# All 22 gate-and-up blocks by seven products, four first halves ahead

## The chip, the cores and the metric

The kernel runs on one core of a Trainium2 chip. The metric is the device time of one execution in microseconds (us). A profile of one execution gives each instruction's engine, start and duration. The engines are PE (TensorE, the matmuls), DVE (VectorE), ACT (ScalarE), POOL (GpSimd) and SP (SyncE, which issues all the DMAs of this kernel). Each engine works through its own instructions in a fixed order and waits for the others by semaphores.

## The reference

One encoder layer over 1024 positions of width 1024, in float32. A long first part (projections, a convolution mixer and a delta-rule mixer) ends in an output projection and a residual add. The change lies in the SwiGLU block that follows:

```python
y = jax.nn.sigmoid(gate_a) * y_conv + jax.nn.sigmoid(gate_b) * y_delta
x = x + y @ w_o[i]

h = rms_norm(x, g_ffn[i])
gt, up = split_cols(h @ w_gate_up[i], (D_FF, D_FF))
x = x + (jax.nn.silu(gt) * up) @ w_down[i]
...
return rms_norm(x, g_final)
```

`D_FF` is 2816, which is 22 blocks of 128 columns each for gate and for up.

## The kernel before

**Tiles.** Activations stand transposed, channels on partitions: `xT[b]` has the 128 channels of block b (8 of them) and 1024 positions, worked on in two halves h of 512. A matmul takes a 128x128 weight and a 128x512 activation. For float32 accuracy every operand is split into a rounded part (hi, a CAST on ACT, L712) and the rest (lo, a subtraction on DVE, L713), and `mm3` (L760) multiplies hi·hi, hi·lo and lo·hi: three matmuls for each 128-deep piece. The third is the one that takes the weight's lo; the second takes the activation's lo.

**Seven products.** A block of gate and up is a 2x2 problem: input channels 0-511 and 512-1023 (r), gate and up columns, times the two position halves. `gate_up` (L1736) does it in a Strassen form, with seven products of weights against the activation forms `B11`, `B21`, `B22`, `T1`, `T2`, `T3`, `T4`, each 4 pieces deep: 7 x 4 x 3 = 84 matmuls. The T forms are running differences of the four quarters of the normalised activation; `sums_of` (L1810) makes a form piece by piece, one DVE subtraction for the difference, then a CAST on ACT and a subtraction on DVE for the split. A plain block (`plain`, L1713) does the same with four products of 8 pieces over `B11`, `B21`, `B12`, `B22`: 96 matmuls, half of them for each position half.

**The beginning of this stage.** The output projection (`wo`, L1634 on) is finished for half 0 first. So `B11` and `B21` (half 0) are ready while `wo` still works on half 1; everything else needs half 1, which becomes available after the last residual add (`resid`, L1608), the norm (`Norm.finish`, L1489, called at L1652) and eight multiplications on DVE (L1656). To bridge this, the kernel before runs the work that needs half 0 alone: `plain(0, 0, ...)`, half of block 0 (48 matmuls), and `first_half` (L1726) of blocks 1 to 3, which are the two products `B11` and `B21` of each (24 matmuls per block). `GU_AHEAD` is the number of such blocks. Then come `plain(0, 1, ...)` with `B12` and `B22` (48 matmuls), the other five products of blocks 1 to 3, and 18 whole blocks. Forms are made on first use:

```python
while acts[0] is None:
    pn.sec = "gu.x"
    sums_of(*coming.pop(0))
    pn.sec = "gu"
```

with `coming` (L1816) in the order T1, T3, B22, T2, T4. In the early blocks the products are taken in that order too (L1741 to L1763).

**Weights.** `part_w` (L1694) loads a 512x128 piece of `w_gate_up` (256 KB) into one of four `raw` or four `rawb` (tile `mid`) buffers; DVE forms sums of the pieces (`s`, `a21`, `a12` in `gate_up`); `split_w` (L1500) splits the result into one of six `w` tiles. So each product has one CAST on ACT and one subtraction on DVE for its weight.

**Order.** `Plan.order` (L347) is a list scheduler with its own table of costs; it runs when the kernel is built, and its result is a fixed order per engine. Lower levels of a key go first, then earlier program order among what it expects to be ready. On the chip nothing is reordered: an instruction whose input is late holds up all that stand behind it on its engine.

Of the kernel before, what the change touches and what calls it, by code (L numbers as in the profile page):

```python
# [576 lines left out]
NS = sum(PAIRS)  # L577
HID_CAP, DF_CAP = 3, 24
GU_BANKS = 8
GU_AHEAD = 3  # L580
OT_AFTER = (4, 7, 10, 12)
WO_AFTER = 13
RE_CAP = 3
# [7 lines left out]
START = (("norm", 0), ("turn", 0, 0, 1), ("rows", 0), ("turn", 0, 1, 8), ("scale", 0, 0, 8),  # L591
         ("norm", 1), ("turn", 1, 0, 1), ("rows", 1), ("turn", 1, 1, 8), ("scale", 1, 0, 8))
PLE_BANKS = (2, 2)
GU_PLAIN = 1
X_AHEAD = 3
LN_KEPT = ()
ROWS_DMA = (0,)
# [27 lines left out]
def hybrid_block(tc, x, p, g_mix, w_in, conv_dw_w, conv_dw_b,  # L625
# [874 lines left out]
    def split_w(src):  # L1500
        t = wp.tile([P, 2, HK, P], F32R, tag="w", line="w", cap=N_W, stream="rest")
        split(t[:, 0], t[:, 1], src)
        return t
# [190 lines left out]
    def part_w(r, c, line):  # L1694

        t = mid.tile([P, HK, P], tag="raw", bufs=4, line=line, cap=4, stream="rest") if line == "raw" else \
            mid.tile([P, HK, P], tag="mid", line=line, cap=4)
        rows_ = w_gate_up[0][r * HK * P:(r + 1) * HK * P, c:c + P]
        pn.dma(t, rows_.rearrange("(k q) c -> q k c", q=P), also=[mark])
        return t  # L1700
# [12 lines left out]
    def plain(fb, h, w, acts):  # L1713

        ps = [gu_bank(), gu_bank()]
        for i in range(2):
            for k in range(KB):
                t = w[2 * i + k // HK]
                mm3(ps[i], t[:, 0, k % HK], t[:, 1, k % HK], *acts[k // HK][k % HK], k == 0, k == KB - 1)
        e = (hid_tile(fb) if h == 0 else hid[fb])[:, h]  # L1720
        pn.act(e, ps[0], AF.Silu)
        pn.tt(e, ps[1], e, ALU.mult)
        if h == 1:
            hidden(fb)

    def first_half(a11, a12):  # L1726

        p1 = mid.tile([P, HW], tag="m2", line="p1", bufs=4)
        pn.act(p1, product(a11, B11))
        yield  # L1730
        g0 = mid.tile([P, HW], tag="lnb", line="g0", bufs=3)
        pn.tt(g0, product(a12, B21), p1, ALU.add)
        pn.act(g0, g0, AF.Silu)
        yield p1, g0
# [64 lines left out]
    ws = []  # L1799
    for fb in range(GU_PLAIN):  # L1800
        ws.append([split_w(part_w(r, c + fb * P, "raw")) for c in (0, FF) for r in range(2)])
        plain(fb, 0, ws[fb], (B11, B21))
    ahead = {}
    for fb in range(GU_PLAIN, GU_PLAIN + GU_AHEAD):
        it = first_half(part_w(0, fb * P, "raw"), part_w(1, fb * P, "rawb"))
# [11 lines left out]

    if GU_PLAIN:
        for k in range(HK):
# [4 lines left out]
        pn.sec = "gu"  # L1824
        for fb in range(GU_PLAIN):
            plain(fb, 1, ws[fb], (B12, B22))
    for fb in range(GU_PLAIN, NF):
        gate_up(fb, ahead.get(fb))
# [231 lines left out]
```

## Time and profile before

| | us |
|---|---|
| median of 3 runs (2058.62 to 2061.99) | 2059.98 |
| the profiled execution | 2064.42 |
| its span, first to last instruction | 2062.7 |
| PE busy | 2032.3 |
| DVE busy | 1593.3 |
| ACT busy | 1115.1 |
| `w_gate_up` loads, first to last issue | 1292.5 to 1685.1 |

Times inside the execution count from the start of the span. A busy share is an average: whether an engine limits a stage is read from the stretch in which it works, and the change concerns a stretch of some 60 us from about 1300 us on. Matmuls overlap in the records: one of 128x512 is recorded with some 400 to 480 ns, and what counts is how often one starts.

### The profile page before, as it was taken

Reading aid. Unit: us, or ns where it says so; the run is one execution under the profiler, and the core shown is the slowest. Engines: PE = TensorE matmul, PEld = TensorE weight load, DVE = VectorE, ACT = ScalarE, POOL = GpSimd, SP = SyncE. Lnnn points to the kernel's source line nnn. Section 1 sums busy time; section 2 is a strip of 40 time slices with the busy share of each in tenths; the row PEclk is TensorE's granted clock in tenths of the full one; section 3 lists DMA queues with packets and bytes.
Section 4 is the critical chain, followed back from the end, with each engine's and each line's share of the span. In section 5 each row is a group of like instructions: output and inputs, shape, how many; then the busy total and the mean of one; then the engine's idle time right before and its main releaser. Section 6 shows DMA issues by size and latency. Waiting matters only on the chain.

```text
span 2062.7 us, 29058 instructions
## 1 busy us (share of the span) xinstructions
PE 2032.3 (99%) x9985; PEld 1670.3 (81%) x9985; DVE 1593.3 (77%) x2814; ACT 1115.1 (54%) x2629; POOL 129.8 (6%) x211
## 2 busy tenths in 40 slices
PE   9999999999999999999999999999999999999998
PEld 6887788888887888888888778888888888887887
DVE  6548999777968999998488876796656657989955
ACT  7635674566766675757875454433333335434462
POOL 1000111001100210012100000000000000000010
PEclk9999999999999999999999999999999999999999
DMA  6432432443333332544488676433323328534232
GB/s 209 153 101 93 133 108 92 147 139 108 118 117 114 111 94 98 189 128 133 159 277 268 206 248 194 143 113 117 98 87 120 100 86 290 165 109 135 85 108 102
DMA packets 278754, 288.61 MB, mean 140 GB/s; under 512 B 17767, under 2 KB 196128, under 8 KB 278606
## 3 DMA queue, kind: packets, MB, share of 16 engines
q1 hardware_dynamic: 278606, 286.76, 43.3%
q8 instruction: 78, 1.28, 0.3%
q14 instruction: 70, 0.57, 0.1%
HBM read 201.16 MB, written 85.53 MB: 139 GB/s over the span
## 4 chain that ended last, share of the span: by engine, by line
PE 51%; DVE 4%; ACT 1%; DMA 1%; issue 1%; SPq 0%; POOLq 0%; DVEq 0%; ACTq 0%
PE ps L244 50%; DVE big L292 2%; ACT big L269 1%; DVE mid L292 1%; DMA big<-d 1%; DMA mid<-d 1%; PE ps L249 0%; DVE w L292 0%; ACT w L269 0%; DVE m L292 0%; SPq L341 0%; DMA d<-mid 0%; ACT big L276 0%; ACT m L276 0%; ACT mid L276 0%
## 5 line engine op out<-in xcount | busy, mean ns | idle before, releaser
L244 PE MATMUL ps<-big,w 128*128 128x512 f32 x6972 | 1708.6, 398 | 4.5 <-ACT big L269 1.6
L244 PEld LDWEIGHTS ps<-big,w 128*128 128x128 f32 x6972 | 1285.4, 188 | 291.7 <-ACT mid L269 6.1
L269 ACT CAST w<-raw 128x512 fp32r<-128x512 f32 (+2 forms) x298 | 176.9, 597 | 258.3 <-PE ps L244 216.9
L292 DVE SCALAR_TENSOR_TENSOR big<-big,taps 128x512 f32<-128x512 f32 (+1 forms) x344 | 300.4, 907 | 12.3 <-ACT big L276 8.3
L292 DVE TENSOR_TENSOR w<-raw,w 128x512 fp32r<-128x512 f32 (+2 forms) x298 | 198.0, 667 | 83.1 <-ACT w L269 81.8
L269 ACT CAST w<-mid 128x512 fp32r<-128x512 f32 (+2 forms) x205 | 113.6, 559 | 145.3 <-PE ps L244 104.4
L292 DVE TENSOR_TENSOR big<-big 128x512 fp32r<-128x512 f32 (+4 forms) x259 | 177.1, 705 | 12.0 <-ACT big L269 5.1
L292 DVE TENSOR_TENSOR w<-mid,w 128x512 fp32r<-128x512 f32 (+2 forms) x205 | 123.9, 609 | 55.9 <-ACT w L269 55.1
L292 DVE TENSOR_TENSOR big<-ps,big 128x512 f32<-128x512 f32 (+1 forms) x172 | 117.4, 686 | 30.3 <-PE ps L244 21.3
L269 ACT CAST big<-big 128x512 fp32r<-128x512 f32 x162 | 95.8, 623 | 48.1 <-DVE big L292 31.1
L269 ACT COPY big<-big 32x128 f32<-32x128 f32 (+1 forms) x264 | 104.5, 443 | 22.7 <-DVE big L292 19.8
L269 ACT COPY big<-ps 128x512 f32<-128x512 f32 (+3 forms) x194 | 83.8, 445 | 54.5 <-PE ps L244 42.9
L244 PEld LDWEIGHTS ps<-big 128*128 128x128 f32 x706 | 99.5, 192 | 16.6 <-issue 5.7
L244 PE MATMUL ps<-big 128*128 128x128 f32 (+2 forms) x706 | 109.2, 299 | 3.1 <-ACT big L269 2.7
L292 DVE SCALAR_TENSOR_TENSOR big<-big,cw31s 128x512 f32<-128x512 f32 x120 | 93.3, 778 | 9.5 <-ACT big L276 7.5
L244 PE MATMUL ps<-w,big 128*128 128x512 f32 (+1 forms) x294 | 80.3, 403 | 0.0
L269 ACT COPY mid<-ps 128x512 f32<-128x512 f32 x72 | 42.0, 587 | 67.7 <-PE ps L244 58.2
L244 PEld LDWEIGHTS ps<-S,big 128*128 128x128 f32 x448 | 68.9, 190 | 10.8 <-DVE S L292 4.5
L244 PE MATMUL ps<-S,big 128*128 128x128 f32 x448 | 77.0, 277 | 0.0
L244 PEld LDWEIGHTS ps<-big,m 128*128 128x128 f32 x512 | 61.5, 191 | 10.2 <-ACT m L276 8.4
L244 PE MATMUL ps<-big,m 128*128 128x128 f32 x512 | 66.1, 279 | 1.0 <-ACT m L276 1.0
L276 ACT ACTIVATE big<-big 128x1024 f32<-128x1024 f32 (+2 forms) x80 | 56.7, 717 | 17.1 <-DVE big L292 13.4
(185 smaller groups left out, 1777.2 us busy)
## 6 DMA issues: line engine op xcount, KB each, us to landing
raw<-in_w_in_dram SPq DMA_DIRECT2D x128, 256.0 KB, 2.9
mid<-d SPq DMA_DIRECT2D x128, 256.0 KB, 3.7
d<-big SPq DMA_DIRECT2D x122, 256.0 KB, 3.2
big<-d SPq DMA_DIRECT2D x118, 256.0 KB, 5.3
d<-mid SPq DMA_DIRECT2D x99, 256.0 KB, 2.2
big<-dqkv SPq DMA_DIRECT2D x32, 512.0 KB, 5.2
raw<-in_w_gate_up_dram SPq DMA_DIRECT2D x49, 256.0 KB, 3.1
dqkv<-big SPq DMA_DIRECT2D x24, 512.0 KB, 2.6
```

The costliest lines, as they stand in the source:

```text
L244: o = self.add("pe", lambda: self.nc.tensor.matmul(out.ap(), lhsT.ap(), rhs.ap(), start=start, stop=stop, **kw), [out], [lhsT, rhs], cost)
L269: return self.nc.scalar.copy(out.ap(), in_.ap())
L276: return self.nc.scalar.activation(out.ap(), in_.ap(), func, **kw)
L292: return getattr(e, name)(**{k: v.ap() if isinstance(v, View) else v for k, v in kw.items()})
```

## The change

Two constants. Block 0 is no longer plain, and four blocks' `first_half` go ahead instead of three.

```diff
-GU_AHEAD = 3
+GU_AHEAD = 4
...
-GU_PLAIN = 1
+GU_PLAIN = 0
```

The loops over `range(GU_PLAIN)` (L1800, L1825) are then empty, `first_half` runs for blocks 0 to 3, `B12` is never made, and `B22` is made when its product in block 0 asks for it (L1823 no longer removes it from `coming`). Blocks 4 to 21 are whole blocks as before. On PE the plain block's 96 matmuls become 84.

What the constants move is told by the order of the built programs. The first place is DVE, about the last residual add (the `SCALAR_TENSOR_TENSOR big<-ps,mid`) and the norm behind it (`nrs`). Before:

```order
L292 SCALAR_TENSOR_TENSOR big<-ps,mid 128x512
L292 TENSOR_TENSOR w<-mid,w 128x512
L292 TENSOR_TENSOR lnb<-lnb,mid 128x512
L292 TENSOR_TENSOR mid<-raw,mid 128x512
L292 TENSOR_TENSOR raw<-raw 128x512
L292 TENSOR_SCALAR nrs<-ps 128x4
```

Now:

```order
L292 TENSOR_TENSOR mid<-raw,mid 128x512
L292 TENSOR_TENSOR raw<-raw 128x512
L292 SCALAR_TENSOR_TENSOR big<-ps,mid 128x512
L292 TENSOR_TENSOR w<-mid,w 128x512
L292 TENSOR_TENSOR lnb<-lnb,mid 128x512
L292 TENSOR_SCALAR nrs<-ps 128x4
L292 TENSOR_TENSOR w<-raw,w 128x512
```

The two weight sums of the first seven-product block (`mid<-raw,mid` is s = a21 + a22) have moved ahead of the residual add, and a weight split stands between `nrs` and the eight multiplications.

The second place is DVE again, from the making of the last pieces of T2 and T4 on (`big<-big`), with `w<-` the weight splits and `ps` results being combined. Before, where T4 is finished:

```order
L292 TENSOR_TENSOR w<-mid,w 128x512
L292 TENSOR_TENSOR big<-big 128x512 x3
L292 TENSOR_TENSOR big<-ps,big 128x512
L292 TENSOR_TENSOR big<-big 128x512 x7
L292 TENSOR_TENSOR mid<-raw,mid 128x512 x2
L292 TENSOR_TENSOR raw<-raw 128x512
L292 TENSOR_TENSOR w<-mid,w 128x512
```

Now (tile `m_13008` is p1 of block 0, into which its products are added):

```order
L292 TENSOR_TENSOR big<-big 128x512
L292 TENSOR_TENSOR big<-ps,big 128x512
L292 TENSOR_TENSOR m_13008<-ps,m_13008 128x512
L292 TENSOR_TENSOR big<-big 128x512
L292 TENSOR_TENSOR m_13008<-ps,m_13008 128x512
L292 TENSOR_TENSOR big<-big 128x512
L292 TENSOR_TENSOR w<-mid,w 128x512
L292 TENSOR_TENSOR big<-big,m_13008 128x512
L292 TENSOR_TENSOR big<-big 128x512
L292 TENSOR_TENSOR raw<-raw 128x512
L292 TENSOR_TENSOR mid<-mid,raw 128x512
L292 TENSOR_TENSOR big<-ps,big 128x512
```

Block 0's combinations now stand between the pieces of T4; before, T4 was made in one stretch and no seven-product block was being combined yet.

The third place is PE, at the end of T4 of the first seven-product block (`w_13225`, sums in `ps_13286`; buffer numbers kept, since the rows would read alike). Now:

```order
L244 MATMUL ps_13286<-big_13280,w_13225 128x512
L244 MATMUL ps_13290<-big_13100,w_13230 128x512 x2
L244 MATMUL ps_13286<-big_13280,w_13225 128x512 x2
L244 MATMUL ps_13286<-big_13288,w_13225 128x512 x3
L244 MATMUL ps_13286<-big_13304,w_13225 128x512 x3
L244 MATMUL ps_13290<-big_13100,w_13230 128x512
L244 MATMUL ps_13286<-big_13315,w_13225 128x512
L244 MATMUL ps_13290<-big_13111,w_13230 128x512 x3
L244 MATMUL ps_13290<-big_13116,w_13230 128x512
L244 MATMUL ps_13286<-big_13315,w_13225 128x512 x2
```

Before, the matmuls at this many places behind the norm belong to the second half of the plain block, in sequence:

```order
L244 MATMUL ps_13279<-big_13035,w_12915 128x512 x3
L244 MATMUL ps_13279<-big_13043,w_12915 128x512 x3
L244 MATMUL ps_13279<-big_13053,w_12915 128x512 x3
L244 MATMUL ps_13279<-big_13063,w_12915 128x512 x3
L244 MATMUL ps_13279<-big_13067,w_12934 128x512 x3
```

Block 1's first late product (T1, into `ps_13290`) is now interleaved with block 0's T4, matmul by matmul.

## The prediction

> **What bounds the kernel now.** First the page's busy shares and its chain that ended last, then that chain about the stage that changes.
>
> ```profile
> span 2062.7 us, 29058 instructions
> PE 2032.3 (99%) x9985; PEld 1670.3 (81%) x9985; DVE 1593.3 (77%) x2814; ACT 1115.1 (54%) x2629; POOL 129.8 (6%) x211
> ...
> 1279.83 140.40 PE ps L244 x618
> ```
>
> PE is busy 99% of the span, and from 1279.83 on the chain is nothing but matmuls for 140 us: through the end of `wo`, the norm, the plain block and the three early blocks PE waits for nobody. So a matmul fewer is a gain, and any new wait of PE is a loss, one for one. Which engine could make PE wait is read from the same stretch cut into slices (busy us of PE, PEld, DVE, ACT, POOL, then the granted clock, DMA share, GB/s):
>
> ```profile
> 1310.00:1320.00 10.00, 10.00 (x53) 8.43 (x52) 6.60 (x12) 3.39 (x6) 1.01 (x1) 1.00 0.19 61
> 1320.00:1330.00 10.00, 10.00 (x45) 8.17 (x44) 10.00 (x18) 5.68 (x11) 0.00 (x0) 1.00 0.24 77
> 1330.00:1340.00 10.00, 10.00 (x46) 8.11 (x45) 10.00 (x17) 7.21 (x13) 0.00 (x0) 1.00 0.21 57
> 1340.00:1350.00 10.00, 10.00 (x45) 8.12 (x44) 10.00 (x18) 5.96 (x11) 0.00 (x0) 1.00 0.36 105
> 1350.00:1360.00 10.00, 10.00 (x45) 8.20 (x44) 10.00 (x17) 3.60 (x6) 0.00 (x0) 1.00 0.07 26
> 1500.00:1600.00 100.00, 100.00 (x434) 80.44 (x433) 61.26 (x93) 36.69 (x63) 0.00 (x0) 1.00 0.33 106
> ```
>
> Here the average misleads. In the whole blocks (1500 to 1600) DVE is busy 61%, but from 1320 to 1360 it has no idle time at all: it makes the forms. PE does not feel it, because it has half-0 work to do meanwhile. DVE is the second bound, hidden behind a cover of matmuls, and the change cuts that cover.
>
> **What is removed.** The plain block's 96 matmuls become 84. The price of one is the pace, not the recorded duration:
>
> ```profile
> 1324.77 50.43 PE L244 MATMUL ps<-big,w 128*128 128x512 f32 x218
> ```
>
> 50.43 / 218 = 0.2313 us, so 12 x 0.2313 = **2.8 us** less on PE, all of it on the chain. The 18 whole blocks, and what follows them, keep their order on PE, so nothing else is gained.
>
> **What is moved: when PE asks for the forms.** The clock of this stage is set by the norm of half 1, which the change leaves alone:
>
> ```profile
> 1309.32 0.69 DVE L292 SCALAR_TENSOR_TENSOR big<-ps,mid 128x512 f32<-128x512 f32 x1 [1.40 <-PE ps L244]
> 1314.41 1.06 PE L244 MATMUL ps<-ident,nrs 128*128 128x128 f32 x8
> 1315.23 11.09 PE L244 MATMUL ps<-big,w 128*128 128x512 f32 x47
> 1316.13 5.39 DVE L292 SCALAR_TENSOR_TENSOR big<-big,vec_t,m 128x512 f32<-128x512 f32 x8 [3.32 <-ACT m L269]
> 1321.43 1.29 DVE L292 TENSOR_TENSOR big<-big 128x512 fp32r<-128x512 f32 x2
> ```
>
> The last residual add is at 1309.32, PE's little norm matmuls end at 1315.23, and DVE is through the eight multiplications at 1321.43. Up to 1315.23 PE has done 19 matmuls of half-0 work by the order (11 ahead of the norm's sums, 8 behind them), before and now. Before, 101 such matmuls were left, and then 48 of the plain block, which need B12 and B22, two forms that DVE makes with one operation per piece; T1 was asked for after 149 matmuls, at 1315.23 + 149 x 0.2313 = 1349.7. Now 96 - 19 = 77 are left, and T1 is asked for at 1315.23 + 77 x 0.2313 = 1333.0: **16.7 us earlier**, while DVE starts on the forms at the same time. T3, B22, T2 and T4 follow at 12 matmuls (2.8 us) each, but a T form costs DVE 8 operations, besides the weight splits and sums.
>
> What DVE needs for one operation:
>
> ```profile
> 1321.43:1355.73 34.30, 34.30 (x151) 27.93 (x150) 34.30 (x58) 20.49 (x37) 0.00 (x0) 1.00 0.24 72
> ...
> 1355.73 1.29 DVE L292 TENSOR_TENSOR mid<-raw,mid 128x512 f32<-128x512 f32 x2
> ```
>
> Between the two rows stand 57 operations (the window counts one more, which began before it): 34.30 / 57 = 0.602 us each, of whatever kind, without a gap; an operation is recorded with 0.69 us, so its result is there 0.69 us after its place begins. What PE then needs is shown where it waited for DVE once before:
>
> ```profile
> 1143.01 0.68 DVE L292 TENSOR_TENSOR w<-mid,w 128x512 fp32r<-128x512 f32 x1
> 1143.75 0.50 PE L244 MATMUL ps<-big,w 128*128 128x512 f32 x1 [0.51 <-DVE w L292]
> ```
>
> 1143.75 - 1143.69 = 0.06 us of hand-over. So the n-th operation behind the multiplications (n from 0, counted in the new order of DVE) is at PE's disposal at 1321.43 + 0.602 n + 0.75, and the m-th matmul after 1315.23 is due at 1315.23 + 0.2313 m. Five places:
>
> - T1's last piece is n = 13: ready 1330.0, due (m = 77 + 10 = 87) 1335.3. In time by 5 us; T3 (n = 23: 1336.0; m = 99: 1338.1) by 2 us.
> - T2's last piece is n = 40: ready 1346.3; due (77 + 36 + 10 = 123) 1343.7. **2.6 us late.**
> - T4's last piece is n = 54, since block 0's combinations stand between its pieces: ready 1354.7; due (142, the order having put seven matmuls of block 1 ahead of it) 1348.1. **6.6 us late.**
> - The weight of block 1's T3 is n = 58: ready 1357.1; due (77 + 48 + 24 + 2 = 151) 1350.2. **6.9 us late.** That of its B22, n = 63: 1360.1 against (164) 1353.2, the same.
> - The weight of block 1's T4 is n = 65: 1361.3 against (187) 1358.5, 2.8 us: by now PE, itself 6.9 us late, is behind DVE.
>
> So the lateness grows to 6.9 us and no further: the forms are made, an early block asks DVE for some 19 operations (11.4 us) per five products (60 x 0.2313 = 13.9 us), and PE is the bound again. That is if DVE never waits. It will a little, for ACT, since a piece is subtraction, CAST, subtraction:
>
> ```profile
> 1320.89 2.71 ACT L269 CAST big<-big 128x512 fp32r<-128x512 f32 x5 [0.70 <-DVE big L292]
> 1328.31 0.62 ACT L269 CAST big<-big 128x512 fp32r<-128x512 f32 x1
> ```
>
> A CAST takes 0.62 us, and the next starts 0.52 us after it. Twice, in T1 and in T3, the new order of ACT has a copy of p1 between two CASTs, and the second piece's lo then comes 0.2 to 0.3 us after its place on DVE. I take 0.5 us for both (bounds: 0, if the copies slip in early; 1.0, if as much again happens in T2 and T4). PE's new wait is thus 6.9 + 0.5 = **7.4 us**, in pieces of up to 2 us between 1342 and 1358, and all of it on the chain.
>
> **What is moved ahead of the residual add.** On DVE the sums `mid<-raw,mid` and `raw<-raw` now stand ahead of the last residual add, on which everything above depends. They wait for a weight load whose buffer comes free with an earlier split:
>
> ```profile
> 1301.75 0.69 DVE L292 TENSOR_TENSOR w<-raw,w 128x512 fp32r<-128x512 f32 x1 [1.25 <-ACT w L269]
> 1307.23 0.69 DVE L292 TENSOR_TENSOR w<-raw,w 128x512 fp32r<-128x512 f32 x1 [1.30 <-ACT w L269]
> ...
> raw<-in_w_gate_up_dram SPq DMA_DIRECT2D x9, 256.0 KB, 4.3
> mid<-in_w_gate_up_dram SPq DMA_DIRECT2D x5, 256.0 KB, 5.9
> ```
>
> The buffer is free at 1302.4; with the 4.3 to 5.9 us to landing of the DMA rows (window 1285 to 1320) the piece is there at 1306.7 to 1308.3. The place for the sums is 1307.9, after the split of 1307.23, and two of them end 1.3 us later, at 1309.2 to 1309.6, where PE releases the residual add at 1309.32. So 0 to 0.3 us, and I take 0. On SP the loads of this stage are 96 instead of 94, and the first `rawb` load has moved ahead of a residual's load; by the order each later load has its buffer at least 3 us before DVE's place for it but one (block 3's s, which has 4 us of slack towards PE). PSUM: the fourth block's first half holds a bank longer, since its `lnb` tile is free only when block 0 is done; seven of eight banks are then in use. I count both at nothing; their price with the cover gone would be a load's 4.3 us.
>
> **Sum.** -2.8 + 7.4 = **+4.6 us** against the profiled execution. That one took 2064.42 us, 1.7 more than its span and 4.4 more than the median of the runs; no row shows where those 4.4 us lie, and I apply the difference to the median: 2059.98 + 4.6 = 2064.6. A measurement of this kernel can tell about 0.2%, 4.1 us, from no change, so the forecast stands just beyond that bound.
>
> **Rivals.**
>
> *A clock step during the waits.* The trace has one place where the granted clock fell inside the span:
>
> ```profile
> 13.18:16.59 3.41, 1.72 (x15) 1.24 (x13) 2.00 (x4) 3.41 (x8) 0.00 (x0) 1.00 1.11 331
> 627.58:630.99 3.41, 1.57 (x9) 0.92 (x7) 1.93 (x7) 3.41 (x16) 0.14 (x2) 1.00 0.43 144
> 630.99:634.40 3.41, 3.41 (x15) 3.11 (x14) 2.15 (x3) 2.65 (x11) 0.00 (x0) 0.50 0.25 68
> ```
>
> After a stretch of 3.4 us with PE busy for 46% it ran at 0.50 for the next 3.4 us; a stretch with 50% (13.18) had no such effect. In my ledger PE is busy for about half of 1351.2 to 1354.6 (six matmuls in three clusters). If the clock falls there, PE starts 7 instead of 15 matmuls in the next 3.4 us, 1.7 us, of which it would have waited 0.2: +1.5 us, net +6.1, **2066.1**. Against it: the share is on the edge, and where such stretches begin is not ours to choose. The Trainium skill, "TensorE: Matmul & The Clock Gate", section "HAM oscillation — how this bites in real kernels", asks only for no idle gap of PE over about 3.4 us; by that rule none of these waits costs any clock and the sum stays at +4.6. The row at 627.58, where PE had begun nine matmuls in the stretch, speaks for the stricter reading.
>
> *The cover suffices (other side).* If DVE's forms came 4.6 us earlier than I have them, the gain would pay for the wait, and with 7.4 us earlier the kernel would win the whole 2.8 us: **2057.2**. The mechanism would be DVE passing its 58 places at 0.602 - 4.6 / 58 = 0.52 us each for break-even, or 0.47 for the whole. No 128x512 operation in the rows does this; only a start of the multiplications before 1316.13 would help, and that waits for PE and POOL in the unchanged norm.
>
> *A shorter wait.* My count lets every lateness of DVE reach PE in full. If only T2's is real (2.6 us) and the rest lies behind matmuls that are ready, the sum is about 0: **2059.8**; between that and the forecast lie the cases in which DVE saves a few places.
>
> *A late load in front of the residual add*, as above with 1 to 2 us in place of 0 to 0.3, shifts the whole ledger: net about +6, **2066**. For it speaks how busy the DMAs are before that residual add:
>
> ```profile
> 1283.00:1311.66 28.66, 28.66 (x128) 23.50 (x126) 21.31 (x35) 13.24 (x23) 0.00 (x0) 1.00 0.81 244
> ```
>
> 81%; against it, the slack worked out above.
>
> **How the numbers follow.** Chances: the forecast (net 3.6 to 5.6 us) 0.50, the clock step 0.17, the late load 0.06, a shorter wait 0.20, the cover suffices 0.05; 0.02 is left. About 0.35 of the forecast's 0.50 lies beyond 4.1 us, so slower 0.35 + 0.17 + 0.06 + 0.01 = 0.59; within 0.2% 0.15 + 0.20 + 0.05 = 0.40 (even the whole 2.8 us is only 0.14%); faster 0.01. The range runs from +1.0 (the lower half of the shorter waits, and the cover, left out) to +7.5 (1.0 us for ACT and the clock step together: 6.9 + 1.0 + 1.5 - 2.8 = 6.6, and a late load of 0.9): 2061.0 to 2067.5.
>
> **What would show it.** Right: PE gap-free to the end of T3, about 1341; then waits of PE for DVE (`w`, `big`) and ACT of some 7 us until about 1358; the whole blocks 4.6 us later than now; DVE with no idle time from 1316 to 1361. Wrong: PE busy throughout (the cover suffices); a residual add after 1309.6 (the load); a clock of 0.50 between 1340 and 1362; a wait of PE in later stages, which I hold to be untouched.

## The result and the profile after

The changed kernel took 2071.41 us in the median of 4 runs (2069.0 to 2074.29), the kernel before 2060.98 us in 4 runs beside it (2058.62 to 2067.01). The ratio is 1.0047 with a 95% interval of 1.0035 to 1.0058: slower by 9.7 us (7.2 to 12.0; the two medians lie 10.4 apart). The forecast was 2064.6, its range ended at 2067.5. The direction was right; the loss is about twice the 4.6 us of the sum. The same program run again in another series (e1_again) gave 1.0037 (1.0024 to 1.0049), that is 7.6 us; the median of that series, 2067.04, lies just inside the range.

The page of the changed kernel, profiled in an execution of 2069.0 us: span and engines.

```profile
span 2067.3 us, 29047 instructions
PE 2034.9 (98%) x9973; PEld 1670.0 (81%) x9973; DVE 1599.3 (77%) x2824; ACT 1113.1 (54%) x2629; POOL 130.0 (6%) x211
```

PE has the 12 matmuls less (9973 against 9985), and is busy 2.6 us **longer**: a matmul at half clock, or one recorded in full because the next has to wait, counts as busy. The averages say nothing of the loss. It is read on PE from the norm of half 1 to the first whole block (the timeline: start, duration, how many matmuls without a gap, and in brackets the idle time ahead of them and what ended it):

```profile
1307.80 1.05 PE L244 MATMUL ps<-ones,lnb 128*128 128x1 f32 x8 [0.79 <-DVE lnb L292]
1308.72 2.10 PE L244 MATMUL ps<-big,w 128*128 128x512 f32 x8
1310.65 1.05 PE L244 MATMUL ps<-ident,nrs 128*128 128x128 f32 x8
1311.46 26.75 PE L244 MATMUL ps<-big,w 128*128 128x512 f32 x114
1338.87 2.09 PE L244 MATMUL ps<-big,w 128*128 128x512 f32 x8 [0.66 <-DVE big L292]
1341.33 0.50 PE L244 MATMUL ps<-big,w 128*128 128x512 f32 x1 [0.37 <-ACT big L269]
1342.48 2.17 PE L244 MATMUL ps<-big,w 128*128 128x512 f32 x8 [0.65 <-DVE big L292]
1344.88 0.73 PE L244 MATMUL ps<-big,w 128*128 128x512 f32 x2 [0.23 <-DVE big L292]
1346.79 0.50 PE L244 MATMUL ps<-big,w 128*128 128x512 f32 x1 [1.17 <-ACT big L269]
1347.88 1.11 PE L244 MATMUL ps<-big,w 128*128 128x512 f32 x2 [0.59 <-DVE big L292]
1349.69 25.68 PE L244 MATMUL ps<-big,w 128*128 128x512 f32 x100 [0.69 <-DVE w L292]
```

Three costs can be read off these rows.

**The waits: 6.8 us.** Behind the norm 114 matmuls run without a gap, through all of T1, T3 and B22 and the first matmul of T2 (77 + 36 + 1 by the order). Then PE waits seven times. Up to the last of these waits 136 matmuls have run; at 0.2313 us each the next would start at 1311.46 + 31.46 = 1342.92. It starts at 1349.69. The idle times in brackets add up to only 4.4 us, since a matmul behind a gap starts when the one ahead has ended and not 0.23 us after its start: a wait costs the bracket and about 0.27 us more (0.50 recorded less the pace).

**The clock: 2.4 us.** The 100 matmuls of the last row take 25.68 us; at the pace they would take 99 x 0.2313 + 0.40 = 23.3. The same stretch by windows (busy us and count of PE, PEld, DVE, ACT, POOL, granted clock, DMA share, GB/s):

```profile
1344.60:1348.03 3.43, 1.43 (x5) 0.63 (x5) 3.43 (x7) 0.62 (x1) 0.00 (x0) 1.00 0.00 0
1348.03:1351.44 3.41, 2.72 (x6) 1.73 (x7) 3.41 (x7) 1.25 (x2) 0.00 (x0) 0.50 0.00 0
1351.44:1354.86 3.42, 3.42 (x9) 2.68 (x9) 1.96 (x4) 0.62 (x1) 0.00 (x0) 0.50 0.26 77
1354.86:1358.30 3.44, 3.44 (x16) 2.79 (x16) 3.44 (x6) 2.21 (x5) 0.00 (x0) 1.00 0.53 170
```

In 1344.60 to 1348.03 PE is busy for 1.43 of 3.43 us, 42%. The clock is 0.50 for the 6.8 us that follow. In the first half of them PE still waits (busy 2.72 of 3.41 us); in the second half it is busy all the time and has 9 matmuls in its records where a full-clock stretch has 16.

**The late load: up to 0.95 us.** DVE about the last residual add, and at the places that the forecast's ledger (its list of DVE's places and PE's due times) spoke of:

```profile
1296.94 0.69 DVE L292 TENSOR_TENSOR w<-raw,w 128x512 fp32r<-128x512 f32 x1 [1.30 <-ACT w L269]
...
1304.27 0.69 DVE L292 TENSOR_TENSOR mid<-raw,mid 128x512 f32<-128x512 f32 x1 [1.16 <-DMA raw<-in_w_gate_up_dram]
1305.00 0.69 DVE L292 TENSOR_TENSOR raw<-raw 128x512 f32<-128x512 f32 x1
1305.61 0.68 DVE L292 SCALAR_TENSOR_TENSOR big<-ps,mid 128x512 f32<-128x512 f32 x1
...
1312.36 5.39 DVE L292 SCALAR_TENSOR_TENSOR big<-big,vec_t,m 128x512 f32<-128x512 f32 x8 [1.30 <-ACT m L269]
1317.66 0.69 DVE L292 TENSOR_TENSOR lnb<-ps,m 128x512 f32<-128x512 f32 x1
...
1350.12 0.72 DVE L292 TENSOR_TENSOR big<-big 128x512 fp32r<-128x512 f32 x1
```

The weight sums that now stand ahead of the residual add waited 1.16 us for their load, the residual add stood behind them, and PE's `ones,lnb` matmuls waited 0.79 us for the sum of squares (first row of PE's timeline). The first operation behind the multiplications (n = 0) starts at 1317.66 and the last piece of T4 (n = 54) at 1350.12: (1350.12 - 1317.66) / 54 = 0.601 us each, as the ledger had it, without a gap on DVE.

To compare runs, the stage is measured on PE's own records, so that what happens ahead of it drops out. That part differs between executions of one program: up to the end of `wo` it took 1309.1 us in the profile of before and 1306.9 in e5_before, 1304.3 in that of the changed kernel and 1301.6 in e1_again. So it is luck that the first two profiled spans lie 2067.3 - 2062.7 = 4.6 us apart, the forecast's very number. The columns: from the end of `wo` to the `ones,lnb` matmuls, from the first matmul behind the norm to the first whole block, the sum of the whole stage, six whole blocks at the same place, and all that follows the stage.

| run | plain block | `wo` end to norm | norm to whole blocks | stage | six whole blocks | rest | 0.50 clock in the stage |
|---|---|---|---|---|---|---|---|
| before | yes | 2.54 | 75.93 | 82.04 | 116.69 | 671.52 | none |
| changed | no | 3.49 | 82.42 | 89.57 | 116.99 | 673.41 | 6.8 us |
| e1_again | no | 2.54 | 81.70 | 87.90 | 116.99 | 673.77 | 3.4 us |
| e2_sums_behind | no | 2.54 | 82.50 | 88.67 | 116.98 | 672.96 | 6.8 us |
| e3_fill | no | 2.81 | 80.80 | 87.26 | 117.02 | 672.89 | none |
| e4_no_diff | no | 2.54 | 76.38 | 82.47 | 116.99 | 673.14 | none |
| e5_before | yes | 2.54 | 75.93 | 82.04 | 116.43 | 671.70 | none |
| e6_plain0_ahead3 | no | 2.54 | 84.76 | 90.85 | 116.97 | 672.50 | 6.8 us |
| e7_plain1_ahead4 | yes | 2.54 | 75.96 | 82.07 | 116.61 | 672.16 | none |
| e8_pool_sums | no | 2.54 | 84.91 | 91.08 | 116.98 | 672.74 | 6.8 us |
| e9_late | no | 2.68 | 81.05 | 87.39 | 116.92 | 673.37 | 3.4 us |
| e10_late_sums | no | 2.54 | 79.70 | 85.87 | 116.94 | 672.41 | 3.4 us |
| e11_shift | no | 3.17 | 82.83 | 89.67 | 116.79 | 672.22 | 6.8 us |
| e12_before_m64 | yes | 2.54 | 76.08 | 82.17 | 116.59 | 671.79 | none |
| e13_before_m32 | yes | 2.54 | 75.93 | 82.04 | 116.58 | 672.13 | none |
| e14_before_shift | yes | 2.53 | 75.80 | 81.90 | 117.00 | 673.84 | none |
| e15_after_m64 | no | 2.54 | 82.46 | 88.57 | 116.92 | 673.19 | 6.8 us |

Each row is one profiled execution. Against the first row, the stage is 7.5 us longer in the first profile of the changed kernel and 5.9 in the second. And the rest, whose order on PE is the same, is longer too, by about 2 us in these two; that was not expected, and the last experiments are about it.

### The profile page after: what moved, and what is told of

It is laid out like the page before. It is cut to its first block, busy times and chain, and to the rows that moved or that the text cites. A ratio compares the mean times of both kernels' runs of the same rounds, so it can differ in the third digit from the quotient of the medians.

```text
span 2067.3 us, 29047 instructions
## 1 busy us (share of the span) xinstructions
PE 2034.9 (98%) x9973; PEld 1670.0 (81%) x9973; DVE 1599.3 (77%) x2824; ACT 1113.1 (54%) x2629; POOL 130.0 (6%) x211
## 4 chain that ended last, share of the span: by engine, by line
PE 46%; DVE 7%; ACT 2%; DMA 1%; issue 1%; SPq 0%; POOLq 0%; DVEq 0%; ACTq 0%
PE ps L244 46%; DVE big L292 4%; ACT big L269 1%; DVE w L292 1%; DMA big<-d 1%; DVE mid L292 1%; PE ps L249 0%; SPq L341 0%; ACT m L276 0%; DMA raw<-in_w_gate_up_dram 0%; DMA big<-dkk 0%; ACT w L269 0%; DVE lnb L292 0%; DVE m L292 0%; ACT mid L276 0%
## 5 line engine op out<-in xcount | busy, mean ns | idle before, releaser
L244 PEld LDWEIGHTS ps<-big,m 128*128 128x128 f32 x512 | 61.5, 191 | 10.1 <-ACT m L276 8.4
```

The lines of the kernel that those rows point to most:

```text
L244: o = self.add("pe", lambda: self.nc.tensor.matmul(out.ap(), lhsT.ap(), rhs.ap(), start=start, stop=stop, **kw), [out], [lhsT, rhs], cost)
```

## The experiments

### The same program again, and the load

**e1_again** is the changed kernel, unedited.

> The changed kernel once more, for its spread and for a second profile. If the loss is made in the ladder of the forms (waits of PE for DVE of 7 us, then a stretch at half clock because of them, and the sums late in front of the residual add), this profile shows all three again between the residual add and block 4, and the median is 9 to 11 us over before. If the half clock was one execution's accident, it is absent here, and the time then stands 2 to 3 us lower than in an execution that has it.

Measured: 2067.04 us (2065.03 to 2069.57, 5 runs), ratio 1.0037 (1.0024 to 1.0049). PE about the last wait, and the clock behind it:

```profile
1304.18 1.05 PE L244 MATMUL ps<-ones,lnb 128*128 128x1 f32 x8
...
1307.84 26.75 PE L244 MATMUL ps<-big,w 128*128 128x512 f32 x114
...
1346.07 29.32 PE L244 MATMUL ps<-big,w 128*128 128x512 f32 x119 [1.06 <-DVE w L292]
```

```profile
1342.70:1346.12 3.42, 1.29 (x4) 0.54 (x4) 3.42 (x7) 1.67 (x3) 0.00 (x0) 1.00 0.00 0
1346.12:1349.53 3.41, 3.41 (x8) 2.74 (x9) 2.30 (x4) 0.62 (x1) 0.00 (x0) 0.50 0.00 1
1349.53:1353.00 3.47, 3.47 (x16) 2.71 (x16) 3.21 (x6) 0.63 (x2) 0.00 (x0) 1.00 0.43 121
```

The first row of PE has no bracket: the load was in time. The waits again cost 6.8 us: 136 matmuls from 1307.84 would end at 1339.30, the next starts at 1346.07. The half clock lasts one stretch of 3.4 us instead of two, and costs 29.32 - (118 x 0.2313 + 0.40) = 1.6 us. So the waits are the same in both executions, while the load (0 or 0.95) and the clock (1.6 or 2.4) are what differs between them. The expectation was met in two of its three causes, and the loss of 7.6 us is less than its 9 to 11.

**e2_sums_behind** puts the first block's weight sums behind the last residual add, by a dependence that only the planner sees (both are DVE operations).

```diff
+    last = [None]
+
     def resid(b, h, ps):
...
         pn.stt(v, ps, 0.5, e, ALU.mult, ALU.add)
+        last[0] = pn.ops[-1]
...
         if early:
             pn.tt(s, a21, a22, ALU.add)
+            pn.ops[-1].deps[last[0]] = True
```

> Only the order on DVE: the two weight sums of block 0 behind the last residual add instead of ahead of it. If their late load holds up the residual add, the PE wait of 0.8 us for lnb goes, the multiplications start 0.8 to 1.0 us earlier after the end of wo, and the kernel is about 1 us faster than the changed one (8 to 10 over before). If the norm has slack there, the time is that of the changed kernel.

Measured: 2069.69 us (2068.62 to 2070.36), 1.0047 (1.0035 to 1.006). The way from `wo` to the norm is 2.54 us as before, so the late load is what the residual add had waited for. But the way from the norm to the whole blocks is 82.50, and the half clock lasted 6.8 us, as in the first profile of the changed kernel. The load was worth up to 0.95 us in an execution; taking it away gains nothing that can be measured, in this form. Over the seven profiles in which the sums stand where the changed kernel has them (changed, e1, e3, e4, e9, e11, e15) the way is 0 to 0.95 us longer, 0.28 in the mean.

### Is it the clock, or DVE's places?

**e3_fill** gives PE 24 matmuls more, three for each piece of T2 and T4, into a bank that nobody reads. They need only the rounded part of the piece, so they run where PE would wait for the rest of it.

```diff
             parted(to_, k, out[k])
+            if to_ is T2 or to_ is T4:
+                pn.level = 1.05
+                for _ in range(3):
+                    ps = ps_.tile([P, HW], tag="ps", line="warm", cap=1)
+                    pn.matmul(ps, to_[k][0][:, :P], to_[k][0], True, True)
+                pn.level = 1
```

> 24 matmuls more (5.5 us of PE), into a bank that nobody reads, three behind each piece of T2 and T4, where PE waits. If PE's idle share is what halves the clock, it stays at full speed between the norm and block 4 and the kernel gains 2 to 2.5 us against the changed one in spite of more work (7 to 8.5 over before). If the half clock costs nothing, because PE would wait for DVE anyway, or comes from something else, the time is the same or up to 2 us longer.

Measured: 2067.19 us (2065.29 to 2068.55), 1.0036 (1.0023 to 1.0048). Windows of the same stretch:

```profile
1342.60:1346.00 3.40, 3.40 (x15) 2.49 (x15) 3.40 (x7) 1.24 (x2) 0.00 (x0) 1.00 0.00 0
1346.00:1349.40 3.40, 3.40 (x16) 2.40 (x14) 3.40 (x6) 0.62 (x1) 0.00 (x0) 1.00 0.00 0
1349.40:1352.80 3.40, 2.34 (x10) 1.62 (x9) 3.40 (x7) 1.36 (x3) 0.00 (x0) 1.00 0.00 0
```

PE is busy up to the last of these windows, the clock stays at 1.00, and the stage is still 5.2 us longer than before (87.26 against 82.04). From the norm to the whole blocks it is 0.9 less than in e1_again; the whole kernel is no faster than e1_again (2067.04), where a gain of 2 to 2.5 us on the changed kernel had been expected. So the clock follows the idle PE, and is the smaller part of the loss. Underneath, DVE is busy in every window, 6 or 7 operations in 3.4 us: the fillers only take the place of waits for it.

**e4_no_diff** leaves the eight differences of T2 and T4 out, so both forms are made of other values than the block needs; every other operation stays.

```diff
-            if b is not None:
+            if b is not None and to_ is not T2 and to_ is not T4:
                 pn.tt(out[k], a[k], b[k], ALU.subtract)
```

> The 8 subtractions of activation quarters for T2 and T4 are left out, so both forms are splits of the quarters themselves and the block's numbers are not the reference's; PE, its products and all splits stay. If the count of DVE operations is the cause, T4 is finished 8 x 0.60 = 4.8 us earlier, PE waits about 2 us instead of 7, the clock does not fall, and the kernel is 7 us faster than the changed one (2 to 4 over before). If PE waits for something else (loads, banks, ACT), the gain is under 2 us.

Measured: 2063.07 us (2060.94 to 2065.37, 11 runs), 1.0018 (1.0009 to 1.0027). The two waits that are left:

```profile
1309.70 34.81 PE L244 MATMUL ps<-big,w 128*128 128x512 f32 x149
1346.22 0.73 PE L244 MATMUL ps<-big,w 128*128 128x512 f32 x2 [1.71 <-ACT w L269]
1347.32 27.89 PE L244 MATMUL ps<-big,w 128*128 128x512 f32 x118 [0.37 <-DVE w L292]
```

Eight operations less on DVE are 4.8 us by the ledger's 0.602. PE now runs 149 matmuls before it waits, the clock does not fall, and the stage is 5.4 us shorter than in e1_again. This is the sharpest test of the ledger: what makes PE wait is how many operations DVE has to do before the piece. (The edit also takes a step out of each piece's own chain; but DVE, without a gap in the changed kernel, was not waiting for that chain.) The half clock goes with it. But the time is still 3.3 us above the 2059.74 of the kernel before in the same series, although the stage is only 0.4 us longer (82.47 against 82.04): the rest is longer by 1.6 than in the first row of the table.

### Which of the two constants?

**e5_before** is the kernel before, unedited; **e6_plain0_ahead3** has GU_PLAIN = 0 with GU_AHEAD = 3; **e7_plain1_ahead4** has GU_PLAIN = 1 with GU_AHEAD = 4.

> The kernel before once more, for a second profile. From the end of wo to the first matmul of the first whole block behind the early ones it took 82.0 us, and 671.5 us from there to the end, where four profiles of the changed order show 673.0 to 673.8. If those 1.4 to 2.2 us belong to the changed program (its whole blocks take 19.50 us each against 19.45), this profile shows 671.5 and 19.45 again; if they are the spread of executions, it shows some 673.

> Only the plain block is taken away; three blocks go ahead as before. T1 is due 24 matmuls (5.55 us) earlier than in the changed kernel, and DVE has three operations fewer ahead of T4 (1.8 us). If cover against DVE's count sets the wait, it grows from 7 to about 10.7 us and the time is 3 to 5 us over the changed kernel's, 10 to 13 over before. If the fourth block ahead, with its bank and its late lnb tile, is what hurts, this kernel is faster than the changed one.

> Only the fourth block ahead; the plain block stays. PE's work is that of before and its cover is 24 matmuls longer, so PE waits nowhere in this stage and the time is that of before, within 1.5 us (a different placement of tiles apart). If a fourth block ahead costs by itself (banks, buffers, DMA), it is 2 us or more over before.

Measured: e5 2060.1 us, 1.0005 (0.9996 to 1.0013); e6 2070.15 (2067.14 to 2073.77), 1.0054 (1.0042 to 1.0066); e7 2059.73 (2057.23 to 2066.87), 1.0002 (0.9991 to 1.0012). In e7 PE runs from the norm into the whole blocks (to the end of the window shown) without a gap:

```profile
1310.48 89.75 PE L244 MATMUL ps<-big,w 128*128 128x512 f32 x388
```

The fourth first half alone changes nothing. Without the plain block and without the fourth first half PE waits from 1329 on, after 69 matmuls:

```profile
1312.08 16.58 PE L244 MATMUL ps<-big,w 128*128 128x512 f32 x69
1329.31 5.22 PE L244 MATMUL ps<-big,w 128*128 128x512 f32 x20 [0.66 <-DVE big L292]
1335.38 0.50 PE L244 MATMUL ps<-big,w 128*128 128x512 f32 x1 [0.84 <-ACT big L269]
```

So the loss belongs to the plain block that is gone, and the fourth first half repays little of it: the cover lost is 48 matmuls of half 0 and 48 that need forms of one DVE operation a piece, and the cover gained is 24.

### Work taken from DVE, or put later

**e8_pool_sums** gives the eight differences to POOL (and the sums behind the residual add, as in e2).

```diff
-                pn.tt(out[k], a[k], b[k], ALU.subtract)
+                pn.tt(out[k], a[k], b[k], ALU.subtract, eng="pool" if to_ is T2 or to_ is T4 else "dve")
```

> The changed kernel with the 8 differences for T2 and T4 made on GpSimd instead of left out or on DVE, and the two sums behind the residual add. If DVE's count is the cause and GpSimd works beside DVE, the wait falls to about 2 us as in the kernel without these differences: 1.5 to 3.5 us over before. If GpSimd is too slow or slows DVE, the time is within 2 us of the changed kernel's.

Measured: 2070.54 us (2068.79 to 2071.6), 1.0055 (1.0042 to 1.0068). POOL's eight operations, the windows, and two of DVE's operations beside POOL:

```profile
1330.78 15.36 POOL L292 TENSOR_TENSOR big<-big 128x512 f32<-128x512 f32 x8 [22.44 <-DVE big L292]
```

```profile
1320.00:1330.00 10.00, 10.00 (x44) 8.10 (x44) 10.00 (x18) 6.69 (x13) 0.00 (x0) 1.00 0.11 30
1330.00:1340.00 10.00, 7.70 (x30) 5.11 (x29) 8.02 (x11) 4.32 (x8) 9.22 (x5) 1.00 0.27 78
1340.00:1350.00 10.00, 5.91 (x14) 4.15 (x15) 10.00 (x10) 3.50 (x7) 6.14 (x4) 0.67 0.00 0
```

```profile
1339.90 1.75 DVE L292 TENSOR_TENSOR big<-big 128x512 fp32r<-128x512 f32 x1
1341.57 1.76 DVE L292 TENSOR_TENSOR mid<-raw,mid 128x512 f32<-128x512 f32 x1
```

POOL takes 15.36 / 8 = 1.92 us for an operation that DVE does in 0.60. And beside POOL's later operations those of DVE start 1.67 us apart (1339.90 to 1341.57) and are recorded with 1.75 us instead of 0.69; in 1340 to 1350, where POOL works for 6.14 us, DVE does 10 operations instead of 18. Both together make this the longest stage of all (91.08). The Trainium skill, "SBUF — State Buffer", section "Who interferes with whom", says that a VectorE instruction with two inputs in SBUF contends with a GpSimd instruction that reads SBUF; by that rule the two hold each other up here, and the 1.67 against 0.60 us agree with it.

**e9_late** leaves nothing out and turns DVE's order: block 0's combinations get a level of 1.05, so they come behind the pieces of the forms and the weight splits.

```diff
+LATE = 1.05
...
             p6 = product(s, T2)
+            pn.level = LATE if fb == 0 else 1
             pn.tt(p1, p6, p1, ALU.add)
...
-            pn.tt(u3, product(a22, T4), u3, ALU.add)
+            pn.level = 1
+            pt = product(a22, T4)
+            pn.level = LATE if fb == 0 else 1
+            pn.tt(u3, pt, u3, ALU.add)
             pn.tt(u3, u3, g0, ALU.mult)
+            pn.level = 1
```

**e10_late_sums** is e9 with the edit of e2.

> The changed kernel with one thing turned: in block 0 the eight operations that combine its products (and the two that follow T4) come behind the form pieces and the weight splits on DVE. Nothing is left out. In its order on DVE T2's last piece is the 36th operation behind the eight multiplications instead of the 40th, T4's last the 44th instead of the 54th, the weight of block 1's T3 the 48th instead of the 58th. Theory A (PE's waits are set by how many places on DVE come before a piece; the half clock is set off by those waits): PE waits 2 to 4 us behind the norm instead of 8.4 to 9.1, no clock of 0.50 there, time 5 to 6 us under the changed kernel's, 2062 to 2065 where the kernel before has 2060. Theory B (the waits come from ACT's CASTs and the load, not from DVE's order): 7 us or more of waits stay, 2067 or more. Theory C (PSUM: block 0's products now hold their banks longer, so block 1's T2 and T4 wait for them): waits move to 1355 to 1362 and the sum stays about 6 us, 2066 or more.

> As e9_late, and the first seven-product block's weight sums also come behind the last residual add. Theory A: as e9_late, and where e9_late's residual add is held up by the late load, 1 us less; otherwise the same within 1 us: 2061 to 2064 where the kernel before has 2060. If e2_sums_behind was slow because the sums then stand among the form pieces (2 to 3 places, 1.2 to 1.8 us), this one is as slow as e9_late or 1 us slower.

Measured: e9 2066.66 us (2063.84 to 2069.66), 1.0029 (1.0018 to 1.0041); e10 2066.24 (2063.98 to 2068.02), 1.0032 (1.0021 to 1.0043). The stage is 0.5 and 2.0 us shorter than in e1_again, not 5. In e9, PE and then the windows about its last wait:

```profile
1348.14 9.24 PE L244 MATMUL ps<-big,w 128*128 128x512 f32 x39 [0.25 <-DVE big L292]
1359.67 15.68 PE L244 MATMUL ps<-big,w 128*128 128x512 f32 x60 [2.29 <-ACT w L269]
```

```profile
1357.43:1360.84 3.41, 1.17 (x5) 1.03 (x6) 3.41 (x7) 1.14 (x2) 0.00 (x0) 1.00 0.79 230
1360.84:1364.25 3.41, 3.41 (x9) 2.66 (x9) 2.37 (x5) 0.05 (x1) 0.00 (x0) 0.50 0.28 78
```

T4's pieces did come earlier, and 39 matmuls ran where the changed kernel waited. Then PE waits 2.29 us for the CAST of a later weight, whose source sum DVE had only just made, and the clock falls behind that wait. In e10 the last wait is for a combination that frees a bank:

```profile
1358.85 16.39 PE L244 MATMUL ps<-big,w 128*128 128x512 f32 x70 [1.41 <-DVE m L292]
```

Theory A was too hopeful: it counted the places ahead of the forms, not the whole backlog. What is put behind the forms falls due here some 10 us later, for a bank or a weight, while DVE is still behind (in e9 it is busy for all of 1344 to 1361). Theory C, the banks, is right for e10 in part. The order decides where PE waits, and how often the clock falls; the length is DVE's.

### The rest of the kernel

Behind the stage the programs without a plain block take 117.0 us for six whole blocks, with one 116.4 to 116.7. Windows inside the whole blocks show it in PE's counts; the first is the kernel before, the second the changed kernel:

```profile
1400.00:1730.00 330.00, 330.00 (x1427) 265.12 (x1426) 200.76 (x304) 119.86 (x204) 0.00 (x0) 1.00 0.35 110
```

```profile
1400.00:1730.00 330.00, 330.00 (x1423) 264.32 (x1422) 201.43 (x305) 119.80 (x204) 0.00 (x0) 1.00 0.34 109
```

PE is busy all the time in both, at full clock, and starts four matmuls fewer. That is 4 x 0.2313 = 0.9 us in 330, and nothing waits. Start to start, most matmuls are 226 to 241 ns apart, in patterns that return in every block. The distances seemed to go with the buffers that the forms lie in: a plain block makes B12, and without it every later form takes another buffer. So the next runs move buffers and keep every order.

**e11_shift** and **e14_before_shift** take and give back four unused buffers just ahead of the forms, in the changed kernel and in the kernel before (four GpSimd fills of 128x4, ordered behind the norm's last GpSimd operation).

```diff
+    turned = [o for o in pn.ops if o.eng == "pool"][-1]
+    for _ in range(4):
+        pad = large(line="pad")
+        pn.fill(pad[:, :4], 0.0)
+        pn.ops[-1].deps[turned] = True
     coming = [(T1, x11, x12, x11), (T3, x12, x22, x12), (B22, x22, x22, None), (T2, x22, x22, x11), (T4, x21, x21, x22)]
```

**e12_before_m64**, **e13_before_m32** and **e15_after_m64** cut two constants (in e13 one), so that all later buffers lie 64 (32) bytes lower.

```diff
-    half16 = const("half16", [P, 16])
+    half16 = const("half16", [P, 8])
...
-    mhalf16 = const("mhalf16", [P, 16])
+    mhalf16 = const("mhalf16", [P, 8])
```

> The changed kernel with every engine's order kept, and four unused buffers taken and given back (four GpSimd fills of 128x4) behind the norm, just ahead of the forms, so that T1, T2, T3, T4 and B22 lie at other addresses; banks and weight buffers as in the changed kernel. Theory P (the whole blocks' pace of 19.50 us in the changed kernel against 19.45 before depends on where the forms lie): the pace moves by 0.02 us or more per block, either way. Theory Q (it depends on the weights, the banks or the order, not on where the forms lie): 117.0 us per six blocks as in all runs without a plain block. In both cases the waits behind the norm stay at 8 to 9 us and the time within 2 us of the changed kernel's.

> The kernel before with two constants (half16, mhalf16) of 8 columns instead of 16: every later buffer lies 64 bytes lower, the order of every engine that takes part is kept, no work in the stage changes. All activation pieces then start at 0 or 128 modulo 256 bytes instead of 64 or 192. In the runs so far matmuls behind each other that read pieces at 64 start 231.4 to 232.2 ns apart, at 192 228.1 to 230.5. Theory P (the address of the pieces sets part of the pace): the whole blocks' pace moves, by more than 0.02 us per block (116.4 to 116.7 us per six blocks before); which way no row tells. Theory Q (the address plays no part): 116.4 to 116.7, and 2060 within 0.2%.

> As e12, with one of the two constants cut: every later buffer lies 32 bytes lower, at 32 or 160 modulo 256. Theory P: the pace moves, not by the same amount as in e12. Theory Q: 116.4 to 116.7 us per six blocks, 2060 within 0.2%.

> The kernel before with four unused buffers taken and given back behind the norm, as in e11: orders kept, forms at other addresses. By the distances that e11 and the other runs show for the same addresses in a row, T3 comes from four pieces of 227 ns to a row of 108864, 75072 and 125760, which took 229 to 238 (about 54 ns more for its 12 matmuls), T1 and T4 lose about 10 ns each: theory P gives 0.03 us more per block, 116.6 to 116.9 us per six blocks, and 2060.5 to 2061.5 in all. Theory Q: 116.4 to 116.7.

> The changed kernel with every later buffer 64 bytes lower, as e12 does to the kernel before. Theory P: its blocks' pace moves the same way as in e12 and the two kernels' whole blocks come within 0.2 us per six blocks of each other if only the address modulo 256 counted; theory Q: 117.0 us per six blocks. The waits behind the norm stay at 8 to 9 us.

Measured: e11 2068.26 us, 1.0039 (1.0026 to 1.0051); e12 2060.56, 1.0002 (0.9993 to 1.0012); e13 2060.37, 1.0001 (0.9992 to 1.001); e14 2061.31 (2060.31 to 2066.48), 1.0008 (0.9999 to 1.0017); e15 2067.34, 1.0038 (1.0025 to 1.0052). The count in e14's whole blocks:

```profile
1400.00:1730.00 330.00, 330.00 (x1423) 264.31 (x1422) 199.93 (x304) 119.75 (x205) 0.00 (x0) 1.00 0.36 113
```

e14 is the clear case: the kernel before, with its order, falls to the changed kernel's 1423 when the forms lie elsewhere, 117.00 us for six blocks, and its rest is the longest of all, 673.84. (Its time alone does not tell it from the kernel before: the interval reaches 0.9999.) The loss is where it was expected: T3's 12 matmuls, whose pieces then lie where the distances had been long, take 2794 ns from start to start instead of 2724 (medians over 14 blocks), 70 more where 54 were expected. e11 goes the other way, 116.79 from 116.99. e12, e13 and e15 leave the pace where it was in their kernel, so it is **not** the address modulo 256; it is which buffers are read after which. Why a row of buffers runs at 227 ns a matmul and another at 232 stays open. That the missing B12 is what sets the changed kernel's pace fits the table (all ten other profiles without it are at 116.92 to 117.02, and e7, with it, is at 116.61), but no run gave the changed kernel the old buffers.

Behind the stage stand 18 whole blocks (17 in e7) and then other products. The 18 blocks took 350.95 us in the mean of the ten profiles without a plain block and with their own buffers, and 349.72 in the four of before, e5, e12 and e13: 1.2 us more. The products behind them took 322.09 and 322.07, the same; yet the profile of before, with 321.59, and that of e5_before, the same program, with 322.37, differ by 0.8 us there. So the 1.2 us lie in the whole blocks, and what the changed kernel's two profiles lose beyond that against the profile of before is spread of executions.

## Why the prediction was right and wrong

**The bound and the cover: right.** PE ran gap-free for 114 matmuls behind the norm, to the point that was forecast (about 1341, some 26 us behind the norm's matmuls; by the forecast's own count that is the end of B22 at m = 113, not that of T3 as it says). Then the waits were for DVE (`big`, `w`) and ACT, in pieces of up to 1.2 us. DVE passed its places at 0.601 us, and T1, T3 and B22 were in time.

**The size of the waits: right, a little high.** Forecast 7.4 us with 0.5 for ACT; measured 6.8 in both profiles. The last wait was for the weight of block 1's T1, which the five places leave out: n = 52 in DVE's order, due at m = 136, by the ledger 1353.5 against 1346.7, 6.8 us late. The 0.5 for ACT did not come, since DVE ran without a gap up to T4's last piece. e4 shows by removal that DVE's operations are what the waits hang on.

**The gain: right.** 2.8 us less on PE; it is in the sum below.

**"I take 0" for the load: the term was mis-sized.** It was between 0 and 0.95 us, 0.28 in the mean, against "0 to 0.3". In the profile of the changed kernel the load's landing took 5.8 us as forecast, but when the buffer came free at 1296.94 + 0.69 = 1297.63, SP issued a store of the residual first (`d<-big`, the first row), and the load went out 0.7 us after the buffer was free. In e1_again that store was already under way when the buffer came free, and the load followed by 0.24 us. The working had left that queue out. From the chain of waits:

```profile
1297.82 0.45 SPq L341
1298.37 5.78 DMA raw<-in_w_gate_up_dram
```

**The clock: the first step that failed.** The forecast was the sum without it, and the step was held at 0.17. It came in 9 of the 11 profiles without a plain block (the other two are e3, which fills the waits, and e4, which leaves work out), and not once in the stage in the 6 with one. The reason given against it was that PE's busy share was on the edge, about half, with six matmuls in the stretch. The waits bunch more than that: in the stretch ahead of the drop PE was busy for 42% (changed) and 38% (e1_again) and began four matmuls (the x5 of the row counts one from ahead of it). Nor was there an edge at half: in e2 and e10 the clock fell behind stretches of 59% and 63% busy. The forecast priced one stretch at 1.5 us; measured were 1.6 for one and 2.4 for two. The Trainium skill's rule, in "TensorE: Matmul & The Clock Gate", section "HAM oscillation — how this bites in real kernels", that asks for no idle gap of PE over some 3.4 us, is not enough here: the longest idle time of PE in the changed kernel's stage is 1.17 us, and the clock was halved for 6.8.

**"18 whole blocks, and what follows them, keep their order on PE, so nothing else is gained": the second step that failed.** The order was kept, the pace was not. The rest took 673.04 us in the mean of the ten programs without a plain block and with their own buffers, 671.86 in the five with one, 1.2 us more, and those lie in the whole blocks; in the two profiles of the changed kernel it was about 2 over the profile of before. Nothing in the prediction allowed for it, and its range ended for that reason where it did: 7.5 us above the kernel before, with clock and load counted in.

The sum, against the kernel before:

| term | forecast | changed | e1_again |
|---|---|---|---|
| matmuls removed | -2.8 | -2.8 | -2.8 |
| waits | 7.4 | 6.8 | 6.8 |
| half clock | 0 | 2.4 | 1.6 |
| late load | 0 | 0.95 | 0 |
| left over in the stage | 0 | 0.2 | 0.3 |
| the rest of the kernel | 0 | 1.9 | 2.2 |
| sum | 4.6 | 9.4 | 8.1 |

The runs say 9.7 (7.2 to 12.0) and 7.6 (4.9 to 10.1). The stage's parts are from single profiles. Of the rest's 1.9 and 2.2 us, 1.0 and 1.1 are the slower pace of the 18 whole blocks, which e14 shows to come with other buffers; the other half lies in the products behind them, which differ nearly as much between two executions of one program.

**The rivals.** The clock step came true, and the late load in one of the two profiles; the shorter wait and the sufficient cover fell. Of the kernels tried none beat the kernel before; e7, e12 and e13 equal it.

## What to carry to other kernels

Before work is taken off the bound engine, count the operations that the hidden engine owes in that stretch, and compare them with the cover that stays: here 12 matmuls saved uncovered 6.8 us of DVE. Waits that let the matmul engine begin only a third of the matmuls that fit into some 3.4 us (3 to 5 of 15 here) should be priced with a half clock behind them, however short each wait is. And a change that takes or frees a buffer can move the pace of matmuls far behind it by some tenths of a per cent, so a result of that size says little of the mechanism until the buffers have been moved by themselves.

## What the runs showed of the hardware

- In the stage the clock fell to 0.50 behind stretches of 3.4 us with PE busy for 29% (e8) to 63% (e10), though no wait of PE there was over 2.4 us; stretches of 52% (e4) and 56% (e8) had no drop behind them. The number of matmuls that began in such a stretch, where some 15 fit (3.41 / 0.2313), sorts them better: with 3 to 5 the clock fell in all eight cases, with 6 in one of three (e10, not e4 nor e8), with 7 or more never. First e4's stretch without a drop, then e10's and what followed:

```profile
1342.70:1346.10 3.40, 1.81 (x8) 1.13 (x6) 3.40 (x7) 1.18 (x3) 0.00 (x0) 1.00 0.11 42
```

```profile
1338.70:1342.10 3.40, 2.15 (x7) 0.97 (x6) 3.40 (x7) 1.86 (x3) 0.00 (x0) 1.00 0.00 0
1342.10:1345.50 3.40, 3.40 (x9) 2.15 (x8) 3.40 (x7) 1.86 (x3) 0.00 (x0) 0.50 0.00 0
```

- The half clock lasted 3.4 us where PE was busy throughout them (e1, e9, e10), and 6.8 us where PE still waited in the first 3.4 (busy for 49% in e8 to 80% in the changed kernel).

- In the whole blocks most matmuls of 128x512 start 226 to 241 ns after the last one, depending on which buffers are read in turn: 12 of them took 2724 ns (T3 in e5_before) or 2794 (T3 in e14_before_shift).
- Eight subtractions of 128x512 on POOL took 1.92 us each, and DVE's operations beside the later ones started 1.67 us apart instead of 0.60.
